# Feed-forward blocks two to four: the plain first chunk becomes one of seven products, two gate chunks are loaded a second time, and the second half of the tokens is turned in one go

## The chip, the cores and the metric

The kernel runs on one core of a Trainium2 chip. The core has five engines with queues of their own: TensorE (PE; its weight loads are listed apart as PEld), VectorE (DVE), ScalarE (ACT), GpSimd (POOL) and SyncE (SP). Each works through its instructions in the order in which the program lists them, and waits for semaphores that other engines or DMAs raise. The metric is the device time of one execution in microseconds (us), from the launch to the end; a version's time is the median of several executions.

## The reference

An encoder of two layers runs over two sequences, of 512 and 256 tokens, with the same weights. Cut to what matters here:

```python
def swiglu_ffn(x, w1, w2):
    gate, up = jnp.split(x @ w1, 2, axis=-1)
    return (jax.nn.silu(gate) * up) @ w2
...
    for li in range(DEPTH):                      # DEPTH = 2
        x = x + 0.5 * swiglu_ffn(rmsnorm(x, norm_g[li, 0]), ffn_w1[li, 0], ffn_w2[li, 0])
        h = rmsnorm(x, norm_g[li, 1])
...
        x = x + mix                              # HGRN2 in layer 0, windowed attention in layer 1
        x = x + 0.5 * swiglu_ffn(rmsnorm(x, norm_g[li, 2]), ffn_w1[li, 1], ffn_w2[li, 1])
    return rmsnorm(x, final_norm_g)
```

The model width is 1024 and the feed-forward width 2816, so `w1` is 1024 x 5632 (gate columns, then up columns) and `w2` is 2816 x 1024. Everything is float32.

## The kernel before

**Token blocks and halves.** The 768 tokens are six blocks of 128, in two halves of 384 (H): blocks 0 to 2 and 3 to 5. `x` stays in SBUF. There are four feed-forward blocks, f0 to f3: f0, the HGRN2 mixer, f1, f2, the attention mixer, f3. The change touches f1, f2 and f3.

**A product in three matmuls.** Each float32 operand is split into a high part, which ACT casts to the matmul's type, and a low part, the rest, which DVE subtracts. A product of two operands is then three matmuls: high by high, high by low, low by high. For tokens that is `split` (cast L320, low part L321); for weights of the first matrix the casts are at L242 and the low parts at L243, 512 elements wide for one operand of a chunk and 1024 for the down projection.

**Chunks and seven products.** The hidden columns are worked off in chunks of 128 gate and 128 up columns. A plain chunk (`up_plain`, matmuls L315 to L317) needs 2 halves x 2 matrices x 8 blocks of the width x 3 = 96 matmuls of 128x384. All other chunks use a scheme of seven products in place of eight: the chunk's weights are a 2 x 2 matrix of blocks (a11 and a12 the two halves of the gate's rows, a21 and a22 those of the up columns), the tokens are another (b00, b10 for the first half of the tokens, b01, b11 for the second), and the products p1 to p7 multiply sums of the one with sums of the other. Each product is 4 x 3 = 12 matmuls of 128x384 (L572, in `product`), a chunk 84. On the token side p1 takes b00, p2 b10, p3 b11, and p4 to p7 take the sums t4, t1, t2 and t3, which `sums` makes once for a block of the model. On the weight side p1 is a11, p2 a12, p4 a22, and p3, p5, p6, p7 are sums of raw weights. p1 + p2 is the gate for the first half of the tokens.

**Groups.** Four chunks make a group, and `down_quad` (matmuls of 128x512, L727) multiplies their results by `w2` in seven products too, 18 matmuls each, and adds them to `x` (`add_x`, L790). Two chunks are left over at the end of a block.

**The start of a block.** A scheduler of the framework then orders each engine's instructions, by the order in the program and by its own estimate of when each can start, so pieces of neighbouring steps are mixed. The norm of the last token blocks of the mixer (or of the block before) is still under way when a feed-forward block starts: DVE scales a token block (L378, `norm_block`), PE turns it with eight transposes (L438, `turn`), ACT evacuates them, and `put` splits them. `turn(half, part, row)` does half of the width for one half of the tokens. It is put into the list `deferred` and called by `run_later` at places between the matmuls. The second half of the tokens is turned while products on the first half run already. So f1 to f3 take their first group in a special order: chunk 0 is plain; chunks 1 and 2 are opened (`open_pair`) with p1 and p2, which need nothing but the first half; then come the rest of `turn`, `sums`, the second half of chunk 0, and the other five products of chunks 1, 2 and 3. The order of a chunk's products is a table, and the order in which its weights are cast follows it:

```python
UP = ("p1", "p7", "p2", "p5", "p4", "p6", "p3")
OPEN = ("p1", "p2", "p3", "p7", "p5", "p6", "p4")
THIRD = ("p1", "p4", "p2", "p7", "p5", "p6", "p3")
```

**Loads of weights.** `load_next` takes the next chunk from `queue` as soon as two of the four raw buffers (`wr`, 512 KB each) are free, and SP issues its DMAs: gate columns, up columns, and another 256 KB of up columns (`s3`). The sums for p7 and p5 are made by DMAs that POOL issues (`into`, L155: the destination plus the source, 256 KB). For p6 and p3, chunks of the order OPEN do the same; others add on DVE (L255). `stage_next` casts and splits the next operand into one of eight `w` buffers (`ahead` runs it forward as buffers come free; `closed` holds it back at marked places).

Of the kernel before, what the change touches and what calls it, by code (L numbers as in the profile page):

```python
# [50 lines left out]
class Trunk:  # L51
    def __init__(self, ctx, tc, consts):
# [14 lines left out]
        self.closed = []  # L67
# [89 lines left out]
    def load_next(self):  # L157
# [11 lines left out]
        if len(raws) == 1:  # L169
            steps = self.plain_steps(key, raws[0], shape)  # L170
        else:
            steps = self.quad_steps(key, raws, srcs, how)
        if how is OPEN and self.opened is None:
            self.loaded.append((2, steps[:2]))
            self.opened = steps[2:]
        elif how is OPEN:
            self.loaded += [(0, steps[:2]), (2, self.opened), (2, steps[2:])]
            self.closed.append(self.loaded[-2])
            self.opened = None
        elif how is THIRD:  # L180
            self.loaded += [(0, steps[:3]), (2, steps[3:])]
            self.closed.append(self.loaded[-1])
        else:
            self.loaded.append((len(raws), steps))
# [4 lines left out]
    def plain_steps(self, key, raw, shape):  # L189
# [20 lines left out]
        return [(2, go)]  # L210

    def quad_steps(self, key, raws, srcs, order):
# [38 lines left out]

        def step(name):
            for into, term in sums.get(name, ()) if order is not OPEN else ():
                with self.tc.issue_after(last[0]):
                    nc.vector.tensor_add(into, into, term)  # L255
            behind = {(OPEN, "p3"): self.turned, (THIRD, "p7"): (self.cast, self.crossed)}.get((order, name))
            if behind:
                cast, low = behind
# [12 lines left out]
    def stage_next(self):  # L271
# [8 lines left out]
        while self.queue and sum(e[0] for e in self.loaded) + len(self.queue[0][1]) <= RAWBUFS:  # L280
            self.load_next()
# [10 lines left out]
    def ahead(self):  # L292
        while self.queue or self.loaded:
            if not self.loaded:
                self.load_next()
            if self.closed and self.loaded[0] is self.closed[0]:
                return
# [3 lines left out]

    def open(self):
        if self.closed:
            self.closed.pop(0)
# [120 lines left out]
    def turn(self, half, part, row):  # L425
# [8 lines left out]
        for m in range(4 * part, 4 * part + 4):  # L434
# [5 lines left out]
            if feeds_ffn:  # L440
                nc.scalar.activation(self.block(part, half, m % 4), pt, AF.Copy, scale=g)
# [5 lines left out]
        for kp in range(2 if feeds_ffn else 0):  # L447
            name = f"b{part}{half}"
            low = self.put(name, kp, self.tn[(part, half)][:, kp])
            self.turned = self.cast, low  # L450
# [27 lines left out]
    def sums(self):  # L478
# [4 lines left out]
        if self.mixed:  # L483
            for kp in range(2):
                self.mix(*(self.tn[(i // 2, i % 2)][:, kp] for i in range(4)), lambda name, src: self.put(name, kp, src))
            return
# [3 lines left out]
        both(lambda kp, b11, b12, b21, b22: (sub(b22, b12, b22), self.put("t3", kp, b22)))  # L490
        both(lambda kp, b11, b12, b21, b22: (sub(b12, b11, b12), self.put("t1", kp, b12)))
        both(lambda kp, b11, b12, b21, b22: (sub(b11, b11, b22), sub(b21, b21, b11), self.put("t2", kp, b11)))
        both(lambda kp, b11, b12, b21, b22: self.put("t4", kp, b21))
# [3 lines left out]
    normal = opened = turned = cast = crossed = None  # L497
    plains = 0

    def after_block(self, b, row):  # L500
# [8 lines left out]
        if half and row % 3 != 1:  # L509
            self.later(self.sums)  # L510

    @staticmethod
    def plain_chunks(tag):
        return 2 if tag == "f0" else 1

    def plan_ffn(self, tag, w1, w2):
        order = {1: OPEN, 2: OPEN, 3: THIRD} if self.plain_chunks(tag) == 1 else {}
# [23 lines left out]
    def up_plain(self, tag, j, half):  # L541
        pss = []
        turns = (((), (2, 6)), ((3, 7), (3, 7)))
        for c in range(2):
# [10 lines left out]
            if half:  # L555
                if not c:
                    self.open()
                self.done((tag, j, c))
# [8 lines left out]
    def product(self, key, name, src, ps, first, last):  # L567
# [13 lines left out]
    def up_pair(self, tag, j, hold=False):  # L581
        nc = self.nc
        third = j == 3 and self.plain_chunks(tag) == 1
        key = (tag, j)
        a, b, c, d = (self.ps(H) for _ in range(4))
        v, w, t = (self.tmp(H) for _ in range(3))
        p = lambda name, ps, first, last: self.product(key, name, FACTOR[name], ps, first, last)
        free = lambda *names: [self.done((*key, name)) for name in names]
        p("p1", a, True, False)
        turned = nc.scalar.copy(v, a).ins  # L590
        free("p1")
        if self.tail:
            self.tail(turned)
        self.tail = None
        p("p4" if third else "p7", c, True, False)
        nc.scalar.copy(w, c)
        free("p4" if third else "p7")
        p("p2", a, False, True)
        nc.scalar.activation(a, a, AF.Silu)
        free("p2")  # L600
        if third:
            p("p7", c, False, True)
            nc.vector.tensor_sub(w, c, w)
            free("p7")
# [3 lines left out]
        if not third:  # L608
            p("p4", c, False, True)
# [22 lines left out]
    def open_pair(self, tag, j, hold):  # L632
# [9 lines left out]
        def free(name):  # L642
            self.done((tag, j, name))
# [1077 lines left out]
```

## Time and profile before

| | |
|---|---|
| median of 3 executions | 2726.7 us (2726.66 to 2726.75) |
| the profiled execution | 2726.4 us, its span 2724.6 us |
| granted clock of TensorE | 0.999 |
| stretch of f1's first group, 993.70 to 1062.00 | PE busy 68.18 of 68.30 us, DVE 61.56, ACT 45.23, POOL 7.83 |
| the same of f2, 1476.70 to 1546.50 | PE 69.42 of 69.80 us, DVE 63.73, ACT 48.29, POOL 7.80 |
| the same of f3, 2226.40 to 2295.80 | PE 69.25 of 69.40 us, DVE 62.84, ACT 48.49, POOL 7.82 |

The span is the time from the first to the last instruction that the profiler recorded, and the execution's own time contains it. Busy time is the union of the engine's instructions in the stretch. A line such as "L378" names the line of the kernel that issued an instruction, and "out<-in" the tiles that it writes and reads.

### The profile page before, as it was taken

To read this page: it belongs to the slowest core of one execution; us is meant where nothing else is said; L and a number is where in the kernel's file an instruction comes from. 1 tells how busy PE (TensorE), PEld (TensorE's weight loads), DVE (VectorE), ACT (ScalarE), POOL (GpSimd) and SP (SyncE) were. 2 spreads that over 40 slices of the span, in tenths; PEclk is the share of its full clock that TensorE was granted. 3 is DMA by queue.
4 is the path that set the end of the run, shared out by engine and by line. 5 is a ranking of instruction groups with operands and counts; after the bars stand their busy time and mean duration, and the time that the engine had idled before them with its cause. 6 is when DMAs were issued, how large, how long until landed. Compare 5 with 4: busy or idle time off the path is not lost.

```text
span 2724.6 us, 44608 instructions
## 1 busy us (share of the span) xinstructions
PE 2715.2 (100%) x17269; PEld 2477.8 (91%) x17269; DVE 2121.7 (78%) x3822; ACT 1346.1 (49%) x2528; POOL 220.1 (8%) x261
## 2 busy tenths in 40 slices
PE   9999999999999999999999999999999999999998
PEld 9999999889888889999999999999987789999998
DVE  8888788567476779778888978887847769788888
ACT  6444444456466564444446544444536755444444
POOL 1110110000000011011111011100000010111000
PEclk9999999999999999999999999999999999999999
DMA  6554554311110435465544455544422124555443
GB/s 184 136 126 115 127 140 124 124 56 48 52 45 25 139 70 147 113 147 128 128 120 105 115 129 139 135 117 113 134 72 78 48 62 116 129 139 135 109 120 108
DMA packets 335588, 299.49 MB, mean 110 GB/s; under 512 B 12088, under 2 KB 260112, under 8 KB 335376
## 3 DMA queue, kind: packets, MB, share of 16 engines
q1 hardware_dynamic: 295936, 213.68, 26.5%
q0 software_dynamic: 35136, 69.48, 14.6%
q10 hardware_dynamic: 4304, 13.49, 1.4%
q8 instruction: 135, 2.21, 0.3%
q14 instruction: 77, 0.63, 0.1%
HBM read 217.70 MB, written 9.44 MB: 83 GB/s over the span
## 4 chain that ended last, share of the span: by engine, by line
PE 98%; DVE 1%; ACT 1%; issue 0%; DVEq 0%; ACTq 0%
PE ps L572 44%; PE ps L727 21%; PE ps L315 8%; PE ps L316 8%; PE ps L317 8%; PE ps L998 1%; PE ps L762 1%; PE ps L1593 1%; PE ps L1584 1%; PE ps L1146 1%; PE ps L1532 1%; PE ps L438 1%; PE ps L1122 0%; PE ps L106 0%; PE ps L1111 0%; PE ps L1518 0%
## 5 line engine op out<-in xcount | busy, mean ns | idle before, releaser
L572 PE MATMUL ps<-big,w 128*128 128x384 f32 x6972 | 1214.1, 334 | 0.0
L572 PEld LDWEIGHTS ps<-big,w 128*128 128x128 f32 x6972 | 1209.5, 188 | 2.4 <-ACT tA L647 0.2
L242 ACT CAST w<-wr 128x512 fp32r<-128x512 f32 (+1 forms) x624 | 434.9, 708 | 716.9 <-DVE wr L255 317.6
L243 DVE TENSOR_TENSOR w<-wr,w 128x512 fp32r<-128x512 f32 (+1 forms) x624 | 492.3, 795 | 214.5 <-ACT w L242 153.4
L727 PE MATMUL ps<-w,big 128*128 128x512 f32 x2520 | 575.7, 389 | 0.0
L727 PEld LDWEIGHTS ps<-w,big 128*128 128x128 f32 x2520 | 472.5, 188 | 98.1 <-DVE x L790 0.4
L790 DVE SCALAR_TENSOR_TENSOR x<-ps,x 128x512 f32<-128x512 f32 x468 | 302.8, 682 | 4.7 <-PE ps L317 4.7
L315 PE MATMUL ps<-w,big 128*128 128x512 f32 x576 | 232.4, 403 | 0.0
L317 PE MATMUL ps<-w,big 128*128 128x512 f32 x576 | 225.4, 391 | 0.0
L316 PE MATMUL ps<-w,big 128*128 128x512 f32 x576 | 225.0, 391 | 0.0
L155 POOL DMA_DIRECT2D s<-wr x125 | 108.8, 911 | 1301.6 <-DMA wr<-in_ffn_w_dram 480.5
L320 ACT CAST big<-tA 128x384 fp32r<-128x384 f32 x296 | 148.0, 513 | 130.8 <-DVE tA L623 40.4
L315 PE MATMUL ps<-big,w 128*128 128x256 f32 (+2 forms) x544 | 185.5, 343 | 0.1
L316 PE MATMUL ps<-big,w 128*128 128x256 f32 (+2 forms) x544 | 183.6, 337 | 0.5 <-DVE big L398 0.2
L317 PE MATMUL ps<-big,w 128*128 128x256 f32 (+2 forms) x544 | 182.9, 336 | 0.0
L155 POOL DMA_DIRECT2D wr<-wr x116 | 100.6, 867 | 984.3 <-DVE tA L1252 385.8
L321 DVE TENSOR_TENSOR big<-tA,big 128x384 fp32r<-128x384 f32 x296 | 160.3, 553 | 8.3 <-ACT big L320 8.2
L202 DVE TENSOR_TENSOR w<-wr,w 128x1024 fp32r<-128x1024 f32 (+1 forms) x82 | 98.7, 1209 | 82.0 <-ACT w L199 73.4
L199 ACT CAST w<-wr 128x1024 fp32r<-128x1024 f32 (+1 forms) x84 | 86.7, 1034 | 93.5 <-PE ps L316 66.3
L315 PEld LDWEIGHTS ps<-w,big 128*128 128x128 f32 x576 | 108.3, 188 | 25.5 <-issue 4.6
L317 PEld LDWEIGHTS ps<-w,big 128*128 128x128 f32 x576 | 108.1, 188 | 23.6 <-issue 0.4
L316 PEld LDWEIGHTS ps<-w,big 128*128 128x128 f32 x576 | 108.4, 188 | 19.6
(207 smaller groups left out, 2869.8 us busy)
## 6 DMA issues: line engine op xcount, KB each, us to landing
wr<-in_ffn_w_dram SPq DMA_DIRECT2D x264, 512.0 KB, 3.9
s<-wr POOLq DMA_DIRECT2D x125, 256.0 KB, 5.3
s<-in_ffn_w_dram SPq DMA_DIRECT2D x123, 256.0 KB, 3.3
wr<-wr POOLq DMA_DIRECT2D x95, 256.0 KB, 4.2
wr<-in_hg_w_in_dram SPq DMA_DIRECT2D x40, 512.0 KB, 3.7
wr<-wr POOLq DMA_DIRECT2D x21, 512.0 KB, 6.1
spill<-x ACTq DMA_DIRECT2D x12, 512.0 KB, 3.8
x<-spill ACTq DMA_DIRECT2D x12, 512.0 KB, 3.2
```

The lines of the kernel that those rows point to most:

```text
L155: self.nc.gpsimd.dma_start(out, src, accum_op=ALU.add)
L202: eng.tensor_sub(lo, raw[:, ks, :], hi.bitcast(F32))
L242: nc.scalar.copy(h, src)
L243: low = nc.vector.tensor_sub(l, src, h.bitcast(F32)).ins
L315: nc.tensor.matmul(out, a[0], b[0], start=first, stop=False)
L316: nc.tensor.matmul(out, a[0], b[1], start=False, stop=False)
L317: nc.tensor.matmul(out, a[1], b[0], start=False, stop=last)
L320: self.cast = self.nc.scalar.copy(hi, src).ins
L321: return self.nc.vector.tensor_sub(lo, src, hi.bitcast(F32)).ins
L572: self.nc.tensor.matmul(ps, a[x], b[y], start=first and k == 0 and i == 0, stop=k == 3 and i == 2, skip_group_check=True,)
L727: nc.tensor.matmul(ps, a[x], w[y], start=name == chain and kp == 0 and q == 0, stop=kp == 1 and q == 2, skip_group_check=True,)
L790: return self.nc.vector.scalar_tensor_tensor(x, ps, c, x, ALU.mult, ALU.add).ins
```

## The change

In f1, f2 and f3:

- Chunk 0 has no plain form any more: it is of seven products, in the order OPEN. Chunk 1 has the same order (NEXT), chunks 2 and 3 the order LATE.
- All four chunks are opened: p1 and p2 of chunks 0, 2, 3 and 1, in this order, run first (`open_gate`). For chunks 2 and 3 the gate columns are loaded by themselves at the start of the block (`gate`, `gate_steps`), and again later with the rest of the chunk, for the other five products. Their results wait in one big tile, `kept`. p1 and p2 of chunk 0 are cast before the gate loads; its other operands stay raw, and it keeps its two raw buffers until then.
- The second half of the tokens is turned in two calls, one after p2 of chunk 0, the other inside p1 of chunk 2, after 6 of its 12 matmuls. The second of them, part 1, when it feeds a feed-forward block, is evacuated on DVE (L454 now) in place of ACT. Operand b01 is not split any more; b11 is split after p1 of chunk 2.
- `sums` keeps only f0's form. For the others `sum_steps` makes the token sums t3, t1, t2 and t4 one after the other, with the casts of chunk 1's weights between.
- The sums of raw weights for p6 and p3 are made by DMA on POOL for all of the four chunks (`more`), where chunk 3 added them on DVE.
- After the opening come p3 and p7 of chunk 0, p3 and p7 of chunk 1, p5 of both, p6 and p4 of chunk 0, then p6 and p4 of chunk 1, and chunks 2 and 3 with p7 p5 p4 p6 p3 (`up_pair` with `opened`).

The diff, cut to its core:

```diff
+GATE = ("p1", "p2")
 OPEN = ("p1", "p2", "p3", "p7", "p5", "p6", "p4")
-THIRD = ("p1", "p4", "p2", "p7", "p5", "p6", "p3")
+NEXT = [*OPEN]
+LATE = ("p7", "p5", "p4", "p6", "p3")
...
-        if len(raws) == 1:
+        if how is GATE:
+            steps = self.gate_steps(key, raws[0])
+        elif len(raws) == 1:
             steps = self.plain_steps(key, raws[0], shape)
         else:
             steps = self.quad_steps(key, raws, srcs, how)
-        if how is OPEN and self.opened is None:
-            self.loaded.append((2, steps[:2]))
-            self.opened = steps[2:]
-        elif how is OPEN:
-            self.loaded += [(0, steps[:2]), (2, self.opened), (2, steps[2:])]
-            self.closed.append(self.loaded[-2])
+        if how is OPEN:
+            at = next((i for i, e in enumerate(self.loaded) if e[2] is GATE), len(self.loaded))
+            self.loaded.insert(at, (0, steps[:2], how))
+            self.opened = (2, steps[2:], how)
+        elif how is NEXT:
+            self.closed = (2, steps[2:], how)
+            self.loaded += [(0, steps[:2], how), self.opened, self.closed]
             self.opened = None
...
-            self.loaded.append((len(raws), steps))
+            self.loaded.append((len(raws), steps, how))
...
+    def gate_steps(self, key, raw):
+        def go(name, half):
+            w = self.wtile()
+            src = raw[:, half * 4 : half * 4 + 4, :]
+            hi, lo = (w[:, i * 512 : (i + 1) * 512].rearrange("p (a b) -> p a b", a=4) for i in range(2))
+            self.split(src, hi, lo)
+            self.staged[(*key, name)] = (hi, lo, 1)
+
+        return [(1, lambda i=i, name=name: go(name, i)) for i, name in enumerate(GATE)]
...
+        def more():
+            for into, term in sums["p6"] + sums["p3"]:
+                self.into(into, term)
+
+        if order is LATE:
+            more()
+
...
+            if order is NEXT and name == "p3" or order is LATE and name == "p7":
+                cast, low = self.summed
                 with self.tc.issue_after(cast), self.tc.issue_after(low):
                     last[0] = split(name, own[name])
             else:
                 last[0] = split(name, own[name])
-            if order is OPEN and name == "p2":
-                for into, term in sums["p6"] + sums["p3"]:
-                    self.into(into, term)
+            if order in (OPEN, NEXT) and name == "p2":
+                more()
...
-                nc.scalar.activation(self.block(part, half, m % 4), pt, AF.Copy, scale=g)
+                if (half, part) == (1, 1) and not self.mixed:
+                    nc.vector.tensor_scalar(self.block(part, half, m % 4), pt, g, None, ALU.mult)
+                else:
+                    nc.scalar.activation(self.block(part, half, m % 4), pt, AF.Copy, scale=g)
...
+            if half and not self.mixed:
+                continue
...
+    def sum_steps(self):
         tiles = [[self.tn[(i // 2, i % 2)][:, kp] for i in range(4)] for kp in range(2)]
...
-        both(lambda kp, b11, b12, b21, b22: (sub(b22, b12, b22), self.put("t3", kp, b22)))
+        low = both(lambda kp, b11, b12, b21, b22: (sub(b22, b12, b22), self.put("t3", kp, b22)))[-1][-1]
+        self.summed = self.gated, low
+        yield
         both(lambda kp, b11, b12, b21, b22: (sub(b12, b11, b12), self.put("t1", kp, b12)))
+        yield
         both(lambda kp, b11, b12, b21, b22: (sub(b11, b11, b22), sub(b21, b21, b11), self.put("t2", kp, b11)))
-        both(lambda kp, b11, b12, b21, b22: self.put("t4", kp, b21))
+        yield
+        low = both(lambda kp, b11, b12, b21, b22: self.put("t4", kp, b21))[-1]
+        self.summed = self.cast, low
+        yield
...
+        def gate(i):
+            self.queue.append(((tag, i), (w1[:, i * P : (i + 1) * P],), (NC, P), GATE))
...
-            if i < self.plain_chunks(tag):
...
-                self.plan_quad((tag, i), (gate, up), (NC, P), order.get(i, UP))
-
+                self.plan_quad((tag, i), (gate, up), (NC, P), UP if first else {0: OPEN, 1: NEXT, 2: LATE, 3: LATE}.get(i, UP))
+
+        if not first:
+            gate(2)
+            gate(3)
...
+            if k == 2 and between:
+                between()
...
+        a, v = opened or (self.ps(H), self.tmp(H))
+        b, c, d = (self.ps(H) for _ in range(3))
...
+        if not opened:
+            p("p1", a, True, False)
+            turned = nc.scalar.copy(v, a).ins
...
+        p("p7", c, True, False)
+        copied = nc.scalar.copy(w, c).ins
+        free("p7")
+        if opened and self.tail:
+            self.tail(copied)
+            self.tail = None
+        if not opened:
...
+    def open_gate(self, tag, j, a, v):
+        nc = self.nc
+        ps = self.ps(H)
+        self.product((tag, j), "p1", FACTOR["p1"], ps, True, False, self.run_later if j == 2 else None)
+        copied = nc.scalar.copy(v, ps).ins
+        self.done((tag, j, "p1"))
+        if j == 2:
+            for kp in range(2):
+                with self.tc.issue_after(copied):
+                    self.put("b11", kp, self.tn[(1, 1)][:, kp])
+        self.product((tag, j), "p2", FACTOR["p2"], ps, False, True)
+        self.gated = nc.scalar.activation(ps if a is None else a, ps, AF.Silu).ins
+        self.done((tag, j, "p2"))
+        if j == 0:
+            self.run_later()
+        return ps if a is None else a, v
...
-                first = [self.up_plain(tag, 0, 0)]
-                put("b00", first[0], 0)
-                gate, p3, p5, p7, p4, p6, results = zip(*(self.open_pair(tag, j, j == 2) for j in (1, 2)))
-                gate[0]()
-                gate[1]()
-                self.take((tag, 1, "p3"))
+                kept = self.big([P, 4, H])
+                opened = {j: self.open_gate(tag, j, *((kept[:, j % 2], kept[:, j]) if j > 1 else (None, self.tmp(H)))) for j in (0, 2, 3, 1)}
+                p3, p7, p5, p6, p4, results = zip(*(self.open_pair(tag, j, *opened[j]) for j in range(2)))
                 self.run_later(len(self.deferred))
-                first.append(self.up_plain(tag, 0, 1))
-                for step in (p3[0], p7[0], p5[0], p6[0], p4[0]):
+                steps = self.sum_steps()
+                for name in ("p3", "p7", "p5"):
+                    next(steps)
+                    self.take((tag, 1, name))
+                for _ in steps:
+                    pass
+                self.closed = self.loaded[1]
+                for step in (p3[0], p7[0], p3[1], p7[1]):
                     step()
+                self.closed = None
+                for step in (p5[0], p5[1], p6[0], p4[0]):
+                    step()
...
                 def second():
-                    for step in (p3[1], p7[1], p5[1]):
-                        step()
-                    self.open()
-                    for step in (p6[1], p4[1]):
-                        step()
+                    p6[1]()
+                    p4[1]()
                     yield from results[1]()
 
-                pairs[0], pairs[1], pairs[2] = first, results[0](), second()
+                pairs = {0: results[0](), 1: second()}
+                pairs.update((j, self.up_pair(tag, j, j == 2, opened[j])) for j in (2, 3))
```

In the changed kernel the same operations have other line numbers: transposes L450, products of 128x384 L594, down projection L751, low parts of weights L254, the scaling of a token block L390, the update of `x` L814. L629 is the line `nc.vector.tensor_sub(w, w, d)` of `up_pair`, L633 to L635 the three behind p6, L707 to L719 stand in `open_pair`.

**PE at the start of f1.** The rows below are of PE before, up to the first transpose of the last token block: `big_9930`, `big_9950` and `big_10013` are the scaled blocks 3, 4 and 5, `ps_10071` the bank of chunk 0's plain up columns.

```order
L438 MATMUL ps_10097<-ident_r,big_9950 128x128
L315 MATMUL ps_10071<-big_9980,w_9843 128x384
L316 MATMUL ps_10071<-big_9980,w_9843 128x384
L317 MATMUL ps_10071<-big_9980,w_9844 128x384
L438 MATMUL ps_10081<-ident_r,big_10013 128x128
```

And of PE now, from the block's first product to the first transpose of block 5: `big_9928`, `big_9948` and `big_10017` are the blocks 3, 4 and 5, `ps_10052` and `ps_10106` the banks of p1 of chunks 0 and 2.

```order
L594 MATMUL ps_10052<-big_9975,w_9833 128x384
L450 MATMUL ps_10085<-ident_r,big_9928 128x128
L450 MATMUL ps_10085<-ident_r,big_9948 128x128
L594 MATMUL ps_10052<-big_9975,w_9833 128x384 x5
L594 MATMUL ps_10052<-big_9978,w_9833 128x384 x6
L450 MATMUL ps_10091<-ident_r,big_9928 128x128
L450 MATMUL ps_10091<-ident_r,big_9948 128x128
L450 MATMUL ps_10096<-ident_r,big_9928 128x128
L450 MATMUL ps_10096<-ident_r,big_9948 128x128
L594 MATMUL ps_10106<-big_9975,w_9847 128x384 x5
L450 MATMUL ps_10085<-ident_r,big_10017 128x128
```

The first transpose of block 5 stood behind 24 products of the plain chunk, of which the last three are shown; it stands now behind the 12 of chunk 0's p1 and the first five of chunk 2's p1.

**DVE around the first low part of chunk 3's weights, in f1.** Before (L662 to L685 are steps of chunks 1 and 2 in `open_pair`; `w_10378` and `w_10395` are operands p1 and p4 of chunk 3, read from raw buffers, `w_10362` is of chunk 2):

```order
L243 TENSOR_TENSOR w_10362<-wr_9849,w_10362 128x512
L662 TENSOR_TENSOR tA_10157<-tA_10157,ps_10331 128x384
L243 TENSOR_TENSOR w_10378<-wr_10286,w_10378 128x512
L676 TENSOR_TENSOR tA_10156<-tA_10156,ps_10381 128x384
L243 TENSOR_TENSOR w_10395<-wr_10288,w_10395 128x512
```

Now (`w_10416` is p7 of chunk 3, `s_1257_10314` the tile in which POOL's DMA makes its sum; L712 to L719 and L707 are the results of chunks 0 and 1):

```order
L254 TENSOR_TENSOR w_10401<-wr_10183,w_10401 128x512
L712 TENSOR_TENSOR tA_10419<-ps_10293,tA_10051 128x384
L254 TENSOR_TENSOR w_10416<-s_1257_10314,w_10416 128x512
L713 TENSOR_TENSOR tA_10419<-tA_10419,ps_10052 128x384
L715 TENSOR_TENSOR tA_10275<-tA_10275,tA_10051 128x384
L707 TENSOR_TENSOR tA_10206<-tA_10206,ps_10429 128x384
```

The first low part of chunk 3 was that of a raw load; it is now that of a sum made by DMA, and the results of chunks 0 and 1 stand behind it on the engine.

More of the change, by code (lines that the diff above doesn't have):

```diff
@@ L250, in quad_steps @@
         last = [None]
+        def more():
[3 more added lines that the diff above has]
+            more()
         def step(name):
-            for into, term in sums.get(name, ()) if order is not OPEN else ():
-                with self.tc.issue_after(last[0]):
+            for into, term in sums.get(name, ()) if order not in (OPEN, NEXT, LATE) else ():
+                with self.tc.issue_after(last[0]) if last[0] else nullcontext():
                     nc.vector.tensor_add(into, into, term)
-            behind = {(OPEN, "p3"): self.turned, (THIRD, "p7"): (self.cast, self.crossed)}.get((order, name))
-            if behind:
-                cast, low = behind
+            if order is NEXT and name == "p3" or order is LATE and name == "p7":
+                cast, low = self.summed
                 with self.tc.issue_after(cast), self.tc.issue_after(low):
@@ L279, in stage_next @@
             self.loaded.pop(0)
-        while self.queue and sum(e[0] for e in self.loaded) + len(self.queue[0][1]) <= RAWBUFS:
+        while self.queue and sum(e[0] for e in (*self.loaded, self.opened or (0,))) + len(self.queue[0][1]) <= RAWBUFS:
             self.load_next()
@@ L508, in after_block @@
         self.later(lambda: self.turn(half, 0, row), lambda: self.turn(half, 1, row))
[L509 to L514, printed above, removed]
     def plan_ffn(self, tag, w1, w2):
-        order = {1: OPEN, 2: OPEN, 3: THIRD} if self.plain_chunks(tag) == 1 else {}
+        first = tag == "f0"
+        def gate(i):
+            self.queue.append(((tag, i), (w1[:, i * P : (i + 1) * P],), (NC, P), GATE))
         def up(i):
             gate, up = (w1[:, c * P : (c + 1) * P] for c in (i, NF + i))
-            if i < self.plain_chunks(tag):
+            if first and i < 2:
                 self.plan((tag, i, 0), gate, (NC, P))
@@ L565, in up_plain, with product @@
         return t
-    def product(self, key, name, src, ps, first, last):
+    def product(self, key, name, src, ps, first, last, between=None):
         wh, wl = self.take((*key, name))
         for k in range(4):
+            if k == 2 and between:
+                between()
             a, b = (wh[:, k, :], wl[:, k, :]), self.operand(src, k)
@@ L579, in product, with up_pair @@
                 )
-    def up_pair(self, tag, j, hold=False):
+    def up_pair(self, tag, j, hold=False, opened=None):
         nc = self.nc
-        third = j == 3 and self.plain_chunks(tag) == 1
         key = (tag, j)
-        a, b, c, d = (self.ps(H) for _ in range(4))
-        v, w, t = (self.tmp(H) for _ in range(3))
+        a, v = opened or (self.ps(H), self.tmp(H))
+        b, c, d = (self.ps(H) for _ in range(3))
+        w, t = (self.tmp(H) for _ in range(2))
         p = lambda name, ps, first, last: self.product(key, name, FACTOR[name], ps, first, last)
         free = lambda *names: [self.done((*key, name)) for name in names]
[L589 to L604, printed above, removed]
+        if not opened:
+            p("p1", a, True, False)
+            turned = nc.scalar.copy(v, a).ins
+            free("p1")
+            if self.tail:
+                self.tail(turned)
+            self.tail = None
[4 more added lines that the diff above has]
+            self.tail(copied)
+            self.tail = None
+        if not opened:
+            p("p2", a, False, True)
+            nc.scalar.activation(a, a, AF.Silu)
+            free("p2")
         p("p5", d, True, False)
@@ L607, in up_pair @@
         free("p5")
-        if not third:
-            p("p4", c, False, True)
+        p("p4", c, False, True)
         p("p6", b, True, True)
@@ L613, in up_pair @@
         nc.vector.tensor_mul(t, t, a)
-        free(*(("p6",) if third else ("p4", "p6")))
+        free("p4", "p6")
         yield t
@@ L804, in ffn @@
             pairs = {}
[L805 removed]
+            if g == 0 and tag == "f0":
                 ts = {}
@@ L849, in ffn @@
                         name = f"b{j}{half}"
-                        if name != "b01" and (n or half):
+                        if name != "b01":
                             put(name, t, kp)
```

54 lines of the change are left out of this document (14 added, 40 removed).

## The prediction

> **What bounds the kernel now.** I read the page's head first, then the chain of waits in order of time, then the timelines of PE, DVE and ACT at the start of the three later feed-forward blocks (f1, f2, f3), and last the DMA table. All times are from the span's start. The head and the chain's shares:
>
> ```profile
> span 2724.6 us, 44608 instructions
> PE 2715.2 (100%) x17269; PEld 2477.8 (91%) x17269; DVE 2121.7 (78%) x3822; ACT 1346.1 (49%) x2528; POOL 220.1 (8%) x261
> PE 98%; DVE 1%; ACT 1%; issue 0%; DVEq 0%; ACTq 0%
> ```
>
> A busy PE need not be a fast PE, so the spacing of the matmuls decides. The chain in order of time, where f1's first group ends (L572 are the feed-forward products of 128x384, L727 those of 128x512 of the down projection; start, length, count):
>
> ```profile
> 1022.39 35.54 PE ps L572 x204
> 1057.93 28.74 PE ps L727 x126
> 1086.66 58.26 PE ps L572 x336
> 1144.93 28.60 PE ps L727 x126
> ```
>
> In an undisturbed group a 128x384 matmul takes 58.26 / 336 = 0.1734 us and a 128x512 one 28.60 / 126 = 0.227. In f1's first group 204 take 35.54, where 204 x 0.1734 = 35.4: hardly 0.2 us of waiting. PE's order is therefore the clock of this kernel: a matmul removed is worth 0.173 us, and every wait that appears on PE is added whole. The stretch from the end of the mixer to the end of f1's first four chunks:
>
> ```profile
> 980.00:1058.00 78.00, 77.88 (x448) 74.63 (x446) 67.87 (x108) 53.45 (x96) 9.55 (x11) 1.00 0.41 96
> ```
>
> The columns after the length are busy time (and count) of PE, PEld, DVE, ACT and POOL, then the granted clock, the DMA share and GB/s. PE is full at clock 1.00; DVE has some 10 us to spare, ACT 24, POOL 68. DVE is second, and works in the order that is written.
>
> **What is removed.** A plain chunk is 2 halves x 2 x 8 x 3 = 96 matmuls of 128x384, a chunk of seven products 7 x 4 x 3 = 84. So 12 go in each of three blocks: 36 x 0.1734 = **6.24 us**, all on the path (2.08 a block). The order of instructions counts the same 36, 7452 against 7416.
>
> **What is added beside PE.** DVE's price is the spacing of starts, since its operations overlap:
>
> ```profile
> 999.96 1.83 DVE L321 TENSOR_TENSOR big<-big,big 128x768 fp32r<-128x768 f32 x2
> ...
> 1013.47 1.82 DVE L491 TENSOR_TENSOR big<-big,big 128x768 f32<-128x768 f32 x2
> 1015.21 0.95 DVE L492 TENSOR_TENSOR big<-big,big 128x768 f32<-128x768 f32 x1
> ...
> 1024.49 2.49 DVE L243 TENSOR_TENSOR w<-wr,w 128x512 fp32r<-128x512 f32 x4
> 1026.90 0.68 DVE L243 TENSOR_TENSOR w<-s,w 128x512 fp32r<-128x512 f32 x1
> ...
> 1047.01 0.55 DVE L682 TENSOR_TENSOR tA<-tA,ps 128x384 f32<-128x384 f32 x1
> 1047.47 0.55 DVE L685 TENSOR_TENSOR tA<-tA,ps 128x384 f32<-128x384 f32 x1
> ...
> 1055.42 1.22 DVE L243 TENSOR_TENSOR w<-wr,w 128x1024 fp32r<-128x1024 f32 x1
> 1056.55 0.55 DVE L611 TENSOR_TENSOR tA<-tA,ps 128x384 f32<-128x384 f32 x1
> ```
>
> That is 1.74 / 2 = 0.87 for 768 elements, 2.41 / 4 = 0.60 for 512, 0.46 for 384 and 1.13 for 1024. By the order, a block gains on DVE seven low parts of weights of 512 (+4.2), four scalings of 384 out of PSUM (+1.85) and four other operations of 384 (+1.85), and loses two low parts of 1024 (-2.3), two splits of 768 (-1.7) and two sums of 512 (-1.2): +2.7 us. The scaling by a column out of PSUM is not in DVE's rows before in this form; the nearest are the 384 rows that read PSUM, so 0.46, and at 1.13 (the 1024 row) it would be 2.7 us more a block. ACT, SP (two loads of 512 KB and one of 256 KB more) and POOL (six sums by DMA more, 0.87 us of issue each) have the room named above. On average nothing of this reaches PE; the 10 us of DVE hide it. Two places are not average.
>
> **First place: the transposes of the last token block.** PE turns the second half of the tokens, with products between; its rows in f1 up to the first transpose of block 5, the half's last, stand with the change above (big_10013 before, big_10017 now). From the block's first product on there were 24 products and 8 transposes ahead of it, now 17 and 8. In f2 it was 24 and 11, now 18 and 9. What it waits for is the scaling of block 5 on DVE (L378). Those scalings and PE's rows with that transpose, f1, f2, f3:
>
> ```profile
> 998.47 0.76 DVE L378 TENSOR_SCALAR big<-x,stat 128x1024 f32<-128x1024 f32 x1
> ...
> 999.28 0.98 PE L438 MATMUL ps<-ident_r,big 128*128 128x128 f32 x7
> ...
> 1486.90 0.75 DVE L378 TENSOR_SCALAR big<-x,stat 128x1024 f32<-128x1024 f32 x1
> ...
> 1487.49 1.03 PE L438 MATMUL ps<-ident_r,big 128*128 128x128 f32 x8
> ...
> 2236.51 0.75 DVE L378 TENSOR_SCALAR big<-x,stat 128x1024 f32<-128x1024 f32 x1
> ...
> 2237.32 0.98 PE L438 MATMUL ps<-ident_r,big 128*128 128x128 f32 x7
> ```
>
> In f1 the scaling ends at 998.47 + 0.76 = 999.23 and PE comes at 999.28: it arrives just in time, without slack. ACT and DVE have the same rows ahead of that scaling before and now (four casts of 512 between), so it does not move, and PE, with seven products less to do, waits 7 x 0.1734 = 1.21 us. f3 is the same (2237.26 against 2237.32); f2 lacks six products and two transposes, again about 1.2. **3.6 us** of the 6.24 go here. The bounds are 0 (if the scaling came earlier for a reason that I don't see) and these 3.6.
>
> **Second place: the weights of chunk 3.** Before, chunk 3 began with p1, which is cast straight from the load. Now its p1 and p2 come from the extra gate load, and it begins with p7, whose operand is a sum made by DMA behind the load. DVE's rows on both sides stand with the change above: w_10378 is that cast's low part before, w_10416 the low part of p7 now, made from the sum s_1257. Sixteen rows behind w_10416 stands L629 on chunk 2 (tA_10493 less ps_10492), which reads a bank into which PE's p3 of chunk 2 then adds; PE waits for it. The time of w_10416, in f1: from 999.96 (b10's low parts, not moved) to the low part of chunk 1's p6, the last but one to free a buffer of raw weights, DVE has 20 operations of 768, 9 of 512 and 4 of 384: 17.4 + 5.4 + 1.85 = 24.7 us, and by following ACT's rows between I get 2.2 us of waits (0 at least, 5 at most): 1026.9. Then chunk 3's load starts. The loads and sums, issue to landing (KB each, median us), the spread of the sums, and before's load and first cast of chunk 3:
>
> ```profile
> wr<-in_ffn_w_dram SPq DMA_DIRECT2D x264, 512.0 KB, 3.9
> s<-wr POOLq DMA_DIRECT2D x125, 256.0 KB, 5.3
> ...
> DMA to landing us min/median/max: 3.2/5.0/8.2
> ...
> 1025.85 0.99 SPq L166 DMA_DIRECT2D wr<-in_ffn_w_dram  x2
> ...
> 1029.86 0.62 ACT L242 CAST w<-wr 128x512 fp32r<-128x512 f32 x1 [2.60 <-DMA wr<-in_ffn_w_dram]
> ```
>
> 1026.9 + 3.9 + 5.3 = 1036.1, the cast 0.6, and a few tenths of hand-over: w_10416 starts at 1037.0. DVE was through with what stands ahead (six of 384, six of 512, 6.4 us) at 1033.3 and idles 3.7. From w_10416 up to L629 are 4 of 512 and 13 of 384: 8.4, so 1045.4. PE, with the first two terms, ends chunk 3 at 1057.93 - 2.08 + 1.21 = 1057.06, and p3 of chunk 2 starts 72 matmuls (12.5 us) earlier, at 1044.6: **0.9 us** of waiting, with the hand-over. The end moves to 1057.96; the down projection's second product would start 18 x 0.227 = 4.1 later, at 1062.05, and needs the first x update (L814). Up to it DVE has 23 of 384, 4 of 1024 and 2 of 512, 16.3 us, plus 0.7 for the sum that p3 of chunk 3 needs: 1062.4, **0.4 us** late. Together 1.3 a block, 3.9 in three. Bounds: with a sum of 3.2 us everything is 2.1 earlier and both waits are gone (0); with 8.2 it is 2.9 later (4.2 a block). I take the median, since 125 sums stand behind it.
>
> A rule speaks against that price. The Trainium skill, "DMA: Bandwidth & Descriptors", Anatomy of one DMA — SWDGE (gpsimd) path, gives a DMA on this path about 2.0 us and its bytes over 436 GB/s. By it a sum of 256 KB would take an estimated 2.6 us, no wait would be left at the second place, and the time would be 2724.3. The 5.3 us of this trace's row disagree, and the sum above goes by the row.
>
> **Sum.** -6.24 + 3.6 + 3.9 = +1.3 on the profiled execution's 2726.4 us, 2727.7. The median of the runs lies 0.3 above it (2726.7), so 2728.0.
>
> **Rivals.** A measurement tells about 0.2% (5.45 us) from no change: faster is below 2721.2, slower above 2732.2.
> - *Nothing waits* (10%): the scaling comes 1.2 us earlier and the sums land fast: 2726.7 - 6.2 = 2720.5. For it speaks DVE's room on average, against it the rows of the first place.
> - *Only the first place waits* (25%): the sums land within about 4 us, as their fastest row allows: 2726.7 - 6.24 + 3.6 = 2724.1.
> - *DVE becomes the bound of the first group* (25%, the slower side): chunk 3's sum lands late, since the next loads now run beside it. At 7.0 us L629 is 1.7 later, the two waits are 3.0, and a block is 1.2 + 3.0 - 2.08 = 2.1 slower: +6.4, 2733.1. It decides from a landing of about 6.7 us, or from as much more work on DVE.
> - That the change doesn't do what it says is no rival: the 36 matmuls are gone in the order.
>
> **How the numbers follow.** 40% for the forecast, 2725.5 to 2731.5, with the second rival 65% for no difference; 10% faster, 25% slower. The range reaches from 2723 to 2734, leaving out the first rival and the upper part of the third.
>
> **What would show it.** Right: in each of the three blocks PE idles about 1.2 us ahead of a transpose, released by DVE's scaling; DVE idles 3 to 4 us ahead of the low part of chunk 3's p7, released by ACT and behind it a DMA; a gap of about 1 us on PE ahead of p3 of chunk 2, released by L629. Wrong: no idle PE at the transposes (then the time falls towards 2720), PE waiting for casts of weights in the gates (a cost that I hold at nothing, since those loads are issued before the block), or a gap at the down projection of over 2 us.

## The result

The change makes the kernel slower: 2751.5 us (median of 5, 2749.7 to 2752.3) against 2726.7, a ratio of 1.009 with a 95% interval of 1.0076 to 1.0105. The forecast was 2728.0 in a range up to 2734. The profiled execution took 2752.3 us. (Behind the medians of x3_dvesum and x6_both below stands one execution each of 6966 us, for which no trace gives a reason; the ratios leave these two out.) The head of its page and the shares of its chain of waits:

```profile
span 2750.3 us, 44655 instructions
PE 2718.1 (99%) x17233; PEld 2477.3 (90%) x17233; DVE 2130.4 (77%) x3849; ACT 1343.5 (49%) x2531; POOL 236.2 (9%) x279
PE 42%; DMA 1%; DVE 1%; ACT 0%; issue 0%; POOL 0%; DVEq 0%; ACTq 0%; POOLq 0%
```

The span grew by 25.7 us. DVE is busy for 8.7 us more and ACT for 2.6 less, so by these totals no engine but PE is full. The chain tells more: it was 98% PE before. Now it can be followed back only to 1532 us, where f2's first group is, so its shares add up to less than half of the span; in f2 and f3 it leaves PE and goes through DMAs and casts. PE's timeline shows where (start, length, operation, count, and in brackets the idle time ahead and what ended it), in f1, f2 and f3:

```profile
1004.14 36.35 PE L594 MATMUL ps<-big,w 128*128 128x384 f32 x206
1047.85 12.26 PE L594 MATMUL ps<-big,w 128*128 128x384 f32 x60 [7.35 <-ACT tA L619]
1060.61 6.53 PE L594 MATMUL ps<-big,w 128*128 128x384 f32 x36 [0.50 <-ACT tA L619]
1066.98 29.24 PE L751 MATMUL ps<-w,big 128*128 128x512 f32 x126
...
1542.56 12.24 PE L594 MATMUL ps<-big,w 128*128 128x384 f32 x60 [4.68 <-ACT tA L619]
1556.46 6.53 PE L594 MATMUL ps<-big,w 128*128 128x384 f32 x36 [1.66 <-ACT tA L619]
...
2301.38 19.67 PE L594 MATMUL ps<-big,w 128*128 128x384 f32 x96 [6.05 <-ACT tA L619]
```

In each block PE stands still once for 4.7 to 7.4 us, 96 matmuls ahead of the down projection: after p7 and p5 of chunk 2, ahead of its p4. p4 adds into the bank that holds p7, and ACT has to copy p7 out of it first; that is L619, `nc.scalar.copy(w, c)`. PE had p7 ready 2 us before it stopped. ACT's timeline in f1 shows why the copy came so late:

```profile
1035.67 0.62 ACT L253 CAST w<-wr 128x512 fp32r<-128x512 f32 x1 [6.95 <-DMA wr<-wr]
1039.45 0.62 ACT L253 CAST w<-s 128x512 fp32r<-128x512 f32 x1 [3.16 <-DMA s<-wr]
1042.84 0.62 ACT L253 CAST w<-wr 128x512 fp32r<-128x512 f32 x1 [2.76 <-DMA wr<-wr]
...
1046.80 0.62 ACT L253 CAST w<-wr 128x512 fp32r<-128x512 f32 x1 [1.32 <-DMA wr<-wr]
1047.33 0.47 ACT L619 COPY tA<-ps 128x384 f32<-128x384 f32 x1
...
1053.59 0.62 ACT L253 CAST w<-wr 128x512 fp32r<-128x512 f32 x1 [4.58 <-DMA wr<-wr]
```

By the order of ACT's instructions the first of these casts is p3 of chunk 2, the next three are p7, p5 and p6 of chunk 3 (p4 between them, at 1043.77), the last is p3 of chunk 3. Each waits for a sum that a DMA makes, and L619 stands behind p6's, on an engine that works in order. ACT is half idle, and PE waits for it. p7's sum needs the gate columns and a load of its own. p5's needs the up columns, whose load took 7.9 us from issue to landing, and behind it the DMAs come one after the other: p6's sum reads what p5's wrote, and p3's what p6's wrote. POOL's issues in f1:

```profile
1028.17 0.87 POOL L156 DMA_DIRECT2D wr<-wr  x1 [2.78 <-DMA wr<-wr]
1031.67 0.86 POOL L156 DMA_DIRECT2D s<-wr  x1 [2.64 <-DVE tA L693]
1036.66 0.86 POOL L156 DMA_DIRECT2D wr<-wr  x1 [4.12 <-ACT w L253]
1043.29 1.78 POOL L156 DMA_DIRECT2D wr<-wr  x2 [5.76 <-issue]
1047.04 0.86 POOL L156 DMA_DIRECT2D wr<-wr  x1 [1.98 <-DMA wr<-wr]
```

From the second row on these are chunk 3's sums for p7, p5, p6 (one of the two at 1043.29; the other is of the down weights) and p3. A second loss hides in the counts: 60 matmuls behind the gap take 12.26 us where 60 x 0.1734 and the tail of the last are 10.6. The view by windows, of the gap and of two stretches behind it, has the granted clock third from the end:

```profile
1040.50:1047.85 7.35, 0.00 (x0) 0.00 (x1) 5.65 (x12) 3.07 (x6) 2.59 (x3) 0.77 0.75 157
...
1049.00:1051.00 2.00, 2.00 (x8) 2.00 (x7) 1.46 (x4) 0.01 (x1) 0.00 (x0) 0.50 0.85 250
...
1053.00:1055.00 2.00, 2.00 (x14) 2.00 (x13) 0.75 (x2) 1.41 (x3) 1.62 (x2) 1.00 0.40 69
```

After the gap PE runs at half clock (8 matmuls in 2 us, later 13 to 14). That costs 1.7, 1.7 and 2.9 us in the three blocks (12.26, 12.24 and 19.67 against 60, 60 and 96 matmuls). The bill: -6.24 for the matmuls, 18.1 for the gaps ahead of p4, 2.2 for those behind them, 6.3 for the clock, and 2.3 more than before at the blocks' start (2.7 against 0.4). That is 22.7 of the 25.7; where the other 3 us went was not traced.

### The profile page after: what moved, and what is told of

Its sections match the earlier page's. It is cut to its first block, busy times and chain, and to the rows that moved or that the text cites. A ratio compares the mean times of both kernels' runs of the same rounds, so it can differ in the third digit from the quotient of the medians.

```text
span 2750.3 us, 44655 instructions
## 1 busy us (share of the span) xinstructions
PE 2718.1 (99%) x17233; PEld 2477.3 (90%) x17233; DVE 2130.4 (77%) x3849; ACT 1343.5 (49%) x2531; POOL 236.2 (9%) x279
## 5 line engine op out<-in xcount | busy, mean ns | idle before, releaser
L594 PE MATMUL ps<-big,w 128*128 128x384 f32 x7224 | 1269.0, 336 | 21.2 <-ACT tA L619 20.2
L594 PEld LDWEIGHTS ps<-big,w 128*128 128x128 f32 x7224 | 1258.5, 189 | 27.0 <-ACT tA L619 21.8
L254 DVE TENSOR_TENSOR w<-wr,w 128x512 fp32r<-128x512 f32 (+1 forms) x630 | 497.2, 795 | 225.7 <-ACT w L253 161.6
L751 PE MATMUL ps<-w,big 128*128 128x512 f32 x2520 | 576.5, 390 | 0.0
L751 PEld LDWEIGHTS ps<-w,big 128*128 128x128 f32 x2520 | 472.3, 188 | 99.1 <-DVE x L814 1.1
L814 DVE SCALAR_TENSOR_TENSOR x<-ps,x 128x512 f32<-128x512 f32 x468 | 303.2, 683 | 4.7 <-PE ps L329 4.6
L156 POOL DMA_DIRECT2D wr<-wr x131 | 113.7, 873 | 1053.9 <-DVE tA L1280 385.8
L327 PE MATMUL ps<-big,w 128*128 128x512 f32 (+2 forms) x448 | 153.3, 342 | 0.1
L328 PE MATMUL ps<-big,w 128*128 128x512 f32 (+2 forms) x448 | 150.9, 337 | 0.2 <-DVE big L410 0.2
L329 PE MATMUL ps<-big,w 128*128 128x512 f32 (+2 forms) x448 | 150.8, 337 | 0.0
L203 DVE TENSOR_TENSOR w<-wr,w 128x1024 fp32r<-128x1024 f32 (+1 forms) x76 | 91.3, 1208 | 76.7 <-ACT w L200 71.1
L254 DVE TENSOR_TENSOR w<-s,w 128x512 fp32r<-128x512 f32 x128 | 87.9, 687 | 38.0 <-ACT w L253 38.0
```

What stands on the lines that cost most here:

```text
L156: self.nc.gpsimd.dma_start(out, src, accum_op=ALU.add)
L203: eng.tensor_sub(lo, raw[:, ks, :], hi.bitcast(F32))
L254: low = nc.vector.tensor_sub(l, src, h.bitcast(F32)).ins
L327: nc.tensor.matmul(out, a[0], b[0], start=first, stop=False)
L328: nc.tensor.matmul(out, a[0], b[1], start=False, stop=False)
L329: nc.tensor.matmul(out, a[1], b[0], start=False, stop=last)
```

## The experiments

Two theories. **Queue**: the weights of chunk 3 come in time for their own products; PE waits because copies that it needs stand on ACT behind casts that wait for DMA sums. **Supply**: the sums come too late for chunk 3, wherever the casts stand. All kernels are compared with the kernel before on the same chip (2726.7 to 2727.1). In their traces line numbers differ by a few; the copy is L616, L621, L625 or L626.

| run | median us | ratio to before, 95% |
|---|---|---|
| the change | 2751.5 | 1.0076 to 1.0105 |
| x1_bar | 2749.9 | 1.0067 to 1.0097 |
| x2_part | 2743.3 | 1.0044 to 1.0078 |
| x3_dvesum | 2735.1 | 1.0017 to 1.0039 |
| x4_act | 2753.5 | 1.0082 to 1.0112 |
| x5_bar2 | 2740.6 | 1.0038 to 1.0064 |
| x6_both | 2730.9 | 1.0006 to 1.0024 |
| x7_all | 2727.7 | 0.9996 to 1.0014 |
| x8_before_dma | 2746.5 | 1.0061 to 1.0087 |
| x9_before_dma | 2732.2 | 1.0012 to 1.0030 |
| x10_mix | 2729.6 | 1.0003 to 1.0021 |

**x1_bar.** Chunk 3 gets an order of its own (LAST), and its casts and low parts get fixed edges: `barred` holds chunk 2's L619 and L629, and the casts come behind the first, the low parts behind the second. The core of it:

```diff
+            elif order is LAST:
+                cast, low = self.barred
+                with self.tc.issue_after(cast), self.tc.issue_after(low):
+                    last[0] = split(name, own[name])
```

> The changed kernel, but the casts of chunk 3's five weight operands on ACT stand behind chunk 2's copy out of PSUM (L619), and their low parts on DVE behind chunk 2's L629. Theory 'queue': PE's gap of 7.35, 4.68 and 6.0 us ahead of chunk 2's p4 is there because L619 stands on ACT behind casts that wait for DMA sums which chunk 2 does not need; then the gap shrinks to under 1 us in each block, the slow stretch of the clock behind it (about 1.85 us a block) goes with it, and the time is 2725 to 2728. Theory 'supply': the weights of chunk 3 come too late in any order; then the gap moves to the first products of chunk 3 and the time stays between 2738 and 2750.

Neither theory had it. The time is that of supply, but the gap is not where supply puts it. PE's timeline in f1 and two rows of ACT's:

```profile
1004.50 46.76 PE L600 MATMUL ps<-big,w 128*128 128x384 f32 x266
1056.60 8.95 PE L600 MATMUL ps<-big,w 128*128 128x384 f32 x36 [5.33 <-ACT tA L625]
...
1052.17 0.62 ACT L254 CAST w<-wr 128x512 fp32r<-128x512 f32 x1 [5.46 <-DMA wr<-wr]
...
1056.07 0.47 ACT L625 COPY tA<-ps 128x384 f32<-128x384 f32 x1
```

PE runs 266 matmuls without a gap, through chunk 2 and the first two products of chunk 3, and then waits again for a copy, that of chunk 3. It stands behind the cast of chunk 3's p3 and, for 3 us more, behind three casts of results and one of down weights. The queue had been cleared at one place and blocked at the next. (The half clock came too: 36 matmuls in 8.95 us.)

**x2_part.** Only the order of the program, no new edges:

```diff
-            if self.loaded[0] is self.closed:
+            if self.loaded[0] is self.closed or self.barred and self.loaded[0][2] is LAST:
                 return
```

> As x1_bar, but without fixed edges: by the order of the program chunk 3's casts come behind L619, and the scheduler still puts the first three of them (p7, p5, p4) ahead of it, so that only the casts of p6 and p3 are behind. Theory 'queue': L619 follows the third cast, which in the changed kernel's trace ends at about 1044, 1539.1 and 2297.3 in place of the fourth at 1047.3, 1542.0 and 2300.9; the gaps become about 4, 1.5 and 2.5 us, and the time 2737 to 2742. Theory 'supply': 2745 to 2752. A reading by DVE alone (L629 held up, as the prediction had it) expects no gain either, since the low parts stay where they were.

The gaps are 3.82 in f1, 2.7 in f2 (1.0 more behind it) and 2.6 us in f3, and the time 1 us above what queue expected. Of the two rows, the first is PE's and the second ACT's copy:

```profile
1044.14 19.71 PE L596 MATMUL ps<-big,w 128*128 128x384 f32 x96 [3.82 <-ACT tA L621]
...
1043.62 0.47 ACT L621 COPY tA<-ps 128x384 f32<-128x384 f32 x1
```

The copy moved ahead by one cast that waits for a DMA, 3.7 us earlier, and PE's gap shrank by 3.5. That is the queue, changed by one step.

**x3_dvesum.** The sums of chunks 2 and 3 for p6 and p3 go back to DVE:

```diff
-        if order is LATE:
-            more()
-            for into, term in sums.get(name, ()) if order not in (OPEN, NEXT, LATE) else ():
+            for into, term in sums.get(name, ()) if order not in (OPEN, NEXT) else ():
```

> The changed kernel, but the sums of raw weights for p6 and p3 of chunks 2 and 3 are additions on DVE (as they were for chunk 3 before), not DMAs on POOL: 12 DMAs fewer in all, 12 additions of 512 more. Theory 'queue': the chain of four DMAs in a row (load, sum of p5, sum of p6, sum of p3) is cut to two, L619 no longer stands behind the third, and chunk 2's own p3 cast no longer holds ACT for 7 us; gaps of 1 to 3 us a block remain, from the sum for chunk 3's p7, and the time is 2730 to 2740. If the DMA sums are not the cause, 2751 or, with the additions on DVE, up to 2757.

16.4 us of the 24.8 come back. The gap ahead of p4 falls to 0.40 us in f1 and 0.38 in f2; f3 keeps 2.86, and DVE's L629 now holds PE for 1.2 to 1.9 us a block. This run alone does not tell the theories apart, since it also takes two of chunk 3's sums out of the row of DMAs.

**x4_act.** The evacuation on ACT again:

```diff
-                if (half, part) == (1, 1) and not self.mixed:
-                    nc.vector.tensor_scalar(self.block(part, half, m % 4), pt, g, None, ALU.mult)
-                else:
-                    nc.scalar.activation(self.block(part, half, m % 4), pt, AF.Copy, scale=g)
+                nc.scalar.activation(self.block(part, half, m % 4), pt, AF.Copy, scale=g)
```

> The changed kernel, but part 1 of the second half of the tokens is evacuated on ACT again (L454 undone). Theory 'queue': the casts that wait for DMAs come 30 us later, so the gap stays as it is and the time is 2750 to 2754. If DVE were the bound of the first group, 1.85 us less on DVE in each block would give 2744 to 2747.

As queue expected: less work on DVE did not help, so DVE's load was not the bound, and this part of the change is not to blame.

**x5_bar2.** x1_bar, and chunk 3's p3 cast behind chunk 3's copy, which is `turned` (the lines are against x1_bar):

```diff
                 cast, low = self.barred
+                if name == "p3":
+                    cast = self.turned
```

> As x1_bar, and the cast of chunk 3's p3 operand stands behind chunk 3's own copy out of PSUM on ACT. In x1_bar PE ran through chunk 2 without a gap and then waited 5.33, 6.2 and 4.6 us ahead of chunk 3's p4 for that copy, which stood behind the p3 cast (it waited 5.46 us for the last DMA sum). Theory 'queue': with the copy ahead, PE waits nowhere over 1 us apart from the start of the block, except at most 1 us ahead of chunk 3's p3 (its sum lands at about 1052.2, PE is there at about 1055.5), and the time is 2725 to 2730. Theory 'supply': the last sum itself is too late; then a gap of 3 us or more stands ahead of chunk 3's p3 and the time is 2737 to 2747.

```profile
1004.48 50.93 PE L604 MATMUL ps<-big,w 128*128 128x384 f32 x290
1055.79 2.35 PE L604 MATMUL ps<-big,w 128*128 128x384 f32 x12 [0.38 <-ACT big L658]
1057.98 4.51 PE L765 MATMUL ps<-w,big 128*128 128x512 f32 x19
1068.02 19.13 PE L765 MATMUL ps<-w,big 128*128 128x512 f32 x83 [2.89 <-DVE x L828]
```

In these rows (PE in f1) the products of the whole first group run through, 290 and 12 of them: supply is refuted, for p3's sum is there in time, with every DMA sum of the change in place. f2 and f3 show the same. But the time expected was wrong by 10 us: the down projection now waits, 2.4 to 2.9 us a block for DVE's first update of `x` and 0.7 to 1.0 for its weights, and in f3 the clock halves behind it. In f1 DVE itself stands still for 3.35 us, up to 1060.60, ahead of the low part of a down weight whose cast on ACT waits 3.75 us for its load; what is left of chunk 3, and the update, stand behind that. In x7_all, which makes chunk 3's last sum on DVE, the same cast starts 2 us earlier in the block, and PE's wait for the update is 0.46 us in f1 and f3 and 1.05 in f2. That the late sum delays the load, by holding its buffer, fits these rows, but was not tested by itself.

**x6_both** and **x7_all** put x3_dvesum's edit into x1_bar and into x5_bar2.

> x1_bar and x3_dvesum together: chunk 3's casts behind chunk 2's copy and the sums for p6 and p3 of chunks 2 and 3 on DVE, so that no cast of chunk 3 behind that of p4 waits for a DMA. Theory 'queue': no gap on PE over 1 us is left apart from the start of the block; DVE, with 2.4 us more work in a block, ends the group 0 to 1 us late; 2724 to 2729. Theory 'supply': as x3_dvesum, 2733 to 2737.

> x5_bar2 and x3_dvesum together. In x6_both the gaps left over 1 us were 2.45 us in f2 and 2.84 in f3 ahead of chunk 3's p4, for chunk 3's copy behind its p3 cast; here that cast stands behind the copy. Theory 'queue': these 5.3 us go, or up to a third of them comes back at the down projection's second product, as DVE is that much later: 2725 to 2728. Theory 'supply': no change from x6_both, 2730 to 2732.

x6 missed by 2 us: 2.45 us in f2 and 2.84 in f3 are left, for chunk 3's copy again. What was expected of x7 puts that down to the p3 cast, and this holds only in part: in f2 the copy (1542.00) stands behind a cast of down weights that waits 1.82 us for its load, in f3 (2294.02) behind the p3 cast, which waits 0.35 us for DVE's addition, and a cast of down weights. x7 puts the copy ahead of all of these, and its time cannot be told from the kernel before. PE's rows in its f1:

```profile
1003.77 53.01 PE L601 MATMUL ps<-big,w 128*128 128x384 f32 x302
1056.62 7.03 PE L762 MATMUL ps<-w,big 128*128 128x512 f32 x29
1064.11 6.20 PE L762 MATMUL ps<-w,big 128*128 128x512 f32 x26 [0.46 <-DVE x L825]
```

302 products without a gap listed. So 23.8 of the 24.8 us are undone with the change's matmuls, loads and opened chunks in place; of the change, the DMA sums for p6 and p3 of chunks 2 and 3 are gone.

**x8_before_dma** and **x9_before_dma** turn it round: the kernel before, with chunk 3's p6 and p3 sums by DMA, in x8 issued with the load, in x9 behind p2's low part. The line of x9:

```diff
-            if order is OPEN and name == "p2":
+            if order in (OPEN, THIRD) and name == "p2":
```

> The kernel before, with one thing of the change: the sums for p6 and p3 of chunk 3 (order THIRD) are made by DMA on POOL as soon as the chunk is loaded, not on DVE. If the DMA sums by themselves cost the time, this is 2732 to 2740. Theory 'queue' with cover: chunk 3 starts with p1, p4 and p2, which are cast straight from the load, so 36 matmuls of 0.1734 us (6.2 us) stand ahead of the first product that needs a sum, and the sums land by about 1047, against a need at 1053.6; at most 1 us a block: 2726 to 2730.

> The kernel before with the sums for p6 and p3 of chunk 3 as DMAs on POOL, issued behind the low part of its p2, so that p1, p4 and p2 are cast straight from the load. (In x8_before_dma the sums were issued with the load and so ran into the operands of p1 and p2: these two read the sums, and their casts waited for them.) Theory 'queue' with cover: the casts of p6 and p3 wait on ACT until about 1041.5 and 1046.5 in f1; what is behind them there is chunk 3's own copy of p4, which PE needs at about 1049.4: 2725 to 2729, while x8, where the first casts of chunk 3 wait, took 2746. If the DMA sums cost the time wherever the casts stand: 2735 or more.

x8 computes p1 and p2 of chunk 3 from the sums in place of the raw weights, so it was not the test that was meant; it is one of the queue all the same. With chunk 3's first cast waiting 6.13 us for a DMA, DVE's low part behind it and DVE's step of chunk 2 (L671) behind that, PE waits 4.13, 2.8 and 3.4 us in a kernel that has nothing else of the change:

```profile
1042.15 1.14 ACT L242 CAST w<-wr 128x512 fp32r<-128x512 f32 x2 [6.13 <-DMA wr<-wr]
...
1045.08 18.49 PE L576 MATMUL ps<-big,w 128*128 128x384 f32 x96 [4.13 <-DVE tA L671]
```

x9 costs 5.6 us, 3 more than queue allowed and 3 less than the other reading asked for. One wait of 2.3 us is plain, in f1: chunk 3's copy of p1 (L590) is behind its p3 cast, which ends its wait of 4.61 us at 1049.29. I had looked at p4's copy, which PE needs later. The other 3 us are not in one place (no other new wait in its trace is over 0.6 us); where they come from stays open.

**x10_mix**: x7_all with chunk 2's sums by DMA.

> x7_all, but the sums for p6 and p3 of chunk 2 are DMAs again and only those of chunk 3 are on DVE. DVE has 1.2 us less in each block, of which up to 1 us may be won at the down projection; against it two DMAs more run beside chunk 3's load, and chunk 2's p3 cast holds ACT until about 1035, when nothing on ACT is wanted by PE. Theory 'queue': 2725 to 2728. Theory 'supply' (the DMAs delay chunk 3's sum): 2730 to 2736.

No gain: 2729.6, between the ranges of the two theories, with 0.5 us ahead of chunk 3's p3 and 1.2 to 1.3 at the down projection in f1 and f2. No version beat the kernel before.

## Why the prediction was wrong

**The matmuls**: right. 36 fewer, and in x7 302 products take 53.01 us, where the spacing assumed gives 52.4.

**First place, 3.6 us**: near in size (2.7 us, 2.3 more than before), but not by the wait that was named, so partly luck. Block 5's scaling did not move (998.63 against 998.47), and PE reaches its transposes at 999.46, just when it ends, in the rows of DVE and PE:

```profile
998.63 0.75 DVE L390 TENSOR_SCALAR big<-x,stat 128x1024 f32<-128x1024 f32 x1
...
997.82 0.44 PE L450 MATMUL ps<-ident_r,big 128*128 128x128 f32 x2 [0.51 <-ACT big L456]
998.48 1.14 PE L594 MATMUL ps<-big,w 128*128 128x384 f32 x5 [0.21 <-ACT big L456]
999.46 0.64 PE L450 MATMUL ps<-ident_r,big 128*128 128x128 f32 x4
```

The time was lost a little earlier, mostly at waits that ACT's evacuations (L456) ended. Without the waits at f1's start (0.89 us) PE would have come to block 5's transposes 0.8 us before the scaling ended, so the wait that was forecast may stand hidden behind these.

**Second place, 3.9 us**: this is the step that failed. It found the right chunk and the right cover that had gone (p1, p4 and p2 no longer stand ahead of the first sum), but it followed DVE's order alone, up to L629, and put ACT down as having "the room named above". Room on average is no room in a queue. PE's first need was ACT's L619, two products before L629 matters, and L619 stood behind a cast that waits for p6's sum. In place of 3.9 us this cost 18.1 us ahead of p4, 2.2 ahead of chunk 3's p4 and 6.3 by the clock, and neither wait of the working appeared: PE's rows list no gap ahead of p3 of chunk 2, nor in the down projection behind it. Of the four sums only p7's was priced; those for p5, p6 and p3, which come in a row, were left to the room on POOL ("0.87 us of issue each" for the added ones). That a wait is "added whole" fell short too, by the 6.3 us of half clock. p7's sum was late as well: w_10416 at 1040.11 where 1037.0 was worked out. Its load started at 1027.06 and took 3.9 us, as priced; the sum took 7.7 in place of 5.3, and the hand-over 0.7. The forecast idle time of DVE is there too (2.63 us ahead of w_10416, and 4.00 ahead of chunk 2's p3, which the working had not), but it was not what held PE. Other loads and sums in that stretch took longer too than the medians of the whole kernel, 3.9 and 5.3:

```profile
wr<-in_ffn_w_dram SPq DMA_DIRECT2D x5, 512.0 KB, 5.4
wr<-wr POOLq DMA_DIRECT2D x6, 256.0 KB, 5.2
s<-in_ffn_w_dram SPq DMA_DIRECT2D x3, 256.0 KB, 4.9
s<-wr POOLq DMA_DIRECT2D x2, 256.0 KB, 5.8
```

(f1 of the change, 1017 to 1048 us.) The rule that the prediction set against its price (the Trainium skill, "DMA: Bandwidth & Descriptors", Anatomy of one DMA — SWDGE (gpsimd) path), an estimated 2.6 us for such a sum, is not borne out here either: the rows have 5.2 and 5.8. The time that it gave by that rule, 2724.3, should be 2724.1 by its own terms.

**The rivals**: the third, late sums, was the nearest, with a sum of 7 us; in f1 it took up to 7.8, from 1031.67 to the cast at 1039.45. But it made DVE the bound, and what held PE was ACT's queue. Its price, 3.0 us of waiting a block, came from the same walk along DVE and was a third of what happened. That x7_all, without the blocked queue, comes to 2727.7, next to the 2728.0 of the forecast, does not bear the sum out: its waits at a block's start and at the down projection stand near where the prediction put them, but its orders and sums are others.

## What to carry to other kernels

Before work is taken from the front of a chunk, ask what it was covering: here 36 matmuls on raw weights hid chunk 3's sums, and the change took the cover away and made the chain behind it longer. Where an engine works in order, an instruction that waits for a DMA holds everything behind it, and the engine's low busy share says nothing about that; walk every queue that the bounding engine waits for, not only the busiest. And clear such a block in one go, since freeing one copy only let PE run to the next.

## What was not expected of the hardware

A stop of PE costs more than its length. After each gap of 3.8 us and more that is quoted here the next matmuls took longer, by 1.7 to 2.9 us in all, and where the granted clock was looked at (the change, x1_bar, x2_part) it was at 0.50 to 0.54 for the first 3 to 6 us. Below 3 us it goes either way. Gaps of 2.56 us (f3 of x2_part), 2.84 (f3 of x6_both) and 2.88 (f3 of x5_bar2) were followed by clocks of 0.50 over 3.1 us, 0.58 over 3.5 and 0.50 over 5.9. Gaps of 2.78 us (f2 of x8_before_dma) and 2.86 (f3 of x3_dvesum) were followed by 1.00, and behind 2.89 us in f1 of x5_bar2 83 matmuls kept their usual time. The Trainium skill, "TensorE: Matmul & The Clock Gate", Part 1: The HAM clock gate, says that the array falls to half rate after an idle window of about 3.4 us and needs as long a busy one to come back. The traces agree on the half rate and on the order of the time, and show three drops after shorter gaps, so 3.4 us is no safe limit here. In the clock records of these runs every such stretch of half clock lasts 3.41 or 6.83 us.
